# Second rows of the residual turned by DVE and DRAM at three stage boundaries

## The chip, the core and the metric

The kernel runs on one core of a Trainium2 chip. TensorE (PE) multiplies matrices from SBUF into PSUM, VectorE (DVE), ScalarE (ACT) and GpSimd (POOL) work on tiles, SyncE (SP) issues DMAs. The metric is the device time of one execution in microseconds (us); lower is better. The kernel before took 928.2 us (median of 3 runs, 925.2 to 928.4).

## What is computed

A trunk of two layers on 256 tokens of width 1024. Each layer adds half a feed-forward block to h, then a mixer (convolution in layer 0, latent attention in layer 1), then half a second feed-forward block. A last norm ends it.

```python
def rmsnorm(x, g):
    return x * lax.rsqrt(jnp.mean(x * x, axis=-1, keepdims=True) + RMS_EPS) * g

def swiglu_ffn(h, w1, w3, w2):
    return (jax.nn.silu(h @ w1) * (h @ w3)) @ w2          # 1024 -> 2816 -> 1024

def mla(h, positions, w_a, g_q, g_kv, w_uq, w_ukv, w_o):
    a = h @ w_a                                            # 1024 -> 512 + 256 + 64
    c_q = rmsnorm(a[..., :Q_LORA], g_q)
    c_kv = rmsnorm(a[..., Q_LORA:Q_LORA + KV_LORA], g_kv)
    k_rope = a[..., Q_LORA + KV_LORA:]
    q = jnp.einsum("bsc,chd->bshd", c_q, w_uq)
    kv = jnp.einsum("bsc,chd->bshd", c_kv, w_ukv)
    ...

for i in range(DEPTH):
    h = h + 0.5 * swiglu_ffn(rmsnorm(h, ffn_norm1[i]), ...)
    m = rmsnorm(h, mix_norm[i])
    h = h + (conv_module(m, ...) if i % 2 == 0 else mla(m, ...))
    h = h + 0.5 * swiglu_ffn(rmsnorm(h, ffn_norm2[i]), ...)
return rmsnorm(h, final_norm)
```

## The kernel before

**Tiles.** The 256 tokens are two row blocks, tb = 0 and 1, of 128 rows ("first rows" and "second rows"). h stands in SBUF with tokens on partitions, h[0] and h[1], each 128 by 1024. A product that sums over the width needs h with channels on partitions, so each stage starts by turning h: eight 128 by 128 tiles a row block, k = 0 to 7. The norm's gain goes in with the turned copy, and its row factor R is applied to the products.

**Products.** Every fp32 product is three fp32r products of a high and a low part (mm3): lo weights with Xh (L251), hi weights with Xh (L254), hi weights with Xl (L255). By names, Xh and Xl are the parts of the turned h, u the products of a feed-forward's first two matrices, o those of its last, a the attention's low-rank products.

**Weights.** SP loads blocks of 1 MB into one of three raw buffers (L162). ACT casts the high part (hi, L167) and DVE subtracts the low part (lo, L168), in two pieces a block, into one of five buffers. load_ahead keeps up to three blocks ahead of use.

**A stage's end.** Rows.finish runs the last two weight blocks as four groups of 12 products, in the order (tb, half of the width) = (0,0), (0,1), (1,0), (1,1). After each group DVE adds the result to h (L513 or L515), and early(i) of the next stage's Norm is called with i = 0 to 3: i = 1 turns the first half of the first rows, i = 2 their second half and starts their row factor, i = 3 turns the first half of the second rows. late() turns the last half and is called in the next stage, after the products of the first rows. A turn is split_rows: four PE transposes into one PSUM buffer of tag B (tp, L295), four ACT copies to Xh (L309), four DVE operations to Xl (L313).

**A stage's start.** The first chunk (c = 0) of ffn_in multiplies with a piece of w1 (m = 0) and of w3 (m = 1), each two weight blocks. m = 0 runs the eight k of the first rows, then the eight of the second; m = 1 follows with both. The attention (mla) starts with low-rank products of two kinds: query (512 wide) for first and second rows, then key and value with rotary key (320 wide) for first and second rows. Each is normed (normed: squares on ACT into junk, L278, powers on POOL, cn on DVE, L1046) and turned into CQ or CK by split_rows; the rotary key kd (key_rope: kx L1051, rp L1001 and L1003) is turned by a PE transpose after the query products qr.

**The gate's way.** The product of silu and gate in ffn_in is already turned without PE: DVE transposes 32 by 32 blocks inside the tile (gt, L558), SP writes four quarters to DRAM (gd, L562) and reads the tile back (gb, L564), in such an order that the blocks land where the whole transpose needs them.

**Order.** Engines work in program order as a scheduler has fixed it; functions marked urgent are put ahead of the surrounding work, and order(a, b) keeps a behind b.

## Time and profile before

| | |
|---|---|
| runs | 928.4, 928.2, 925.2 us; median 928.2 |
| profiled execution | 925.73 us; its span 923.9 us; mean granted clock 0.998 |
| weight DMA, 1 MB | 5.0 us from issue to landing (median) |
| HBM | 206 GB/s over the span |

The page gives for each engine its busy time and share of the span. The chain of waits follows back from the last instruction to what released it. Rows of groups read: line, engine, operation, output <- input, shapes, count, then busy us and mean ns of one, then the engine's idle time just before them with what ended it. Rows of the timeline read: start, length, engine, line, operation, and in brackets the idle time before. Rows by stretch read: window, length, then busy us and count of PE, PEld (weight loads), DVE, ACT and POOL, then the granted clock, DMA share and GB/s. A row of waits reads: instruction waiting <- instruction waited for, total us, times, longest.

The edited boundaries lie at about 450 to 470 us (end of layer 0's second feed-forward, start of layer 1's first), 632 to 652 (into the attention) and 733 to 746 (out of the attention).

### The profile page before, as it was taken

Reading aid. Unit: us, or ns where it says so; the run is one execution under the profiler, and the core shown is the slowest. Engines: PE = TensorE matmul, PEld = TensorE weight load, DVE = VectorE, ACT = ScalarE, POOL = GpSimd, SP = SyncE. Lnnn points to the kernel's source line nnn. Section 1 sums busy time; section 2 is a strip of 40 time slices with the busy share of each in tenths; the row PEclk is TensorE's granted clock in tenths of the full one; section 3 lists DMA queues with packets and bytes.
Section 4 is the critical chain, followed back from the end, with each engine's and each line's share of the span. In section 5 each row is a group of like instructions: output and inputs, shape, how many; then the busy total and the mean of one; then the engine's idle time right before and its main releaser. Section 6 shows DMA issues by size and latency. Waiting matters only on the chain.

```text
span 923.9 us, 12098 instructions
## 1 busy us (share of the span) xinstructions
PE 914.5 (99%) x4370; PEld 767.5 (83%) x4370; DVE 585.3 (63%) x925; ACT 493.4 (53%) x844; POOL 120.1 (13%) x255
## 2 busy tenths in 40 slices
PE   9999999999999999999999999999999999999997
PEld 7888888898978888888888888888898888888886
DVE  5895764489987666654476665544676686556633
ACT  7664443488877444543465444534666574445422
POOL 1720000079941000000000000001200000000000
PEclk9999999999999999999999999999999999999999
DMA  9886776534227767766457776753451567676711
GB/s 336 312 311 234 279 245 226 183 138 137 93 69 281 244 231 245 251 217 222 178 190 253 244 244 234 252 183 120 182 183 46 201 232 245 232 247 241 242 46 46
DMA packets 60972, 191.58 MB, mean 207 GB/s; under 512 B 11376, under 2 KB 33520, under 8 KB 41584
## 3 DMA queue, kind: packets, MB, share of 16 engines
q1 hardware_dynamic: 60336, 190.13, 58.8%
q8 instruction: 34, 0.56, 0.2%
q10 hardware_dynamic: 576, 0.69, 0.2%
q14 instruction: 26, 0.21, 0.1%
HBM read 178.20 MB, written 12.58 MB: 206 GB/s over the span
## 4 chain that ended last, share of the span: by engine, by line
PE 91%; DVE 5%; ACT 2%; issue 1%; POOL 1%; DMA 0%; POOLq 0%; ACTq 0%; DVEq 0%
PE u L251 17%; PE u L254 17%; PE u L255 17%; PE o L255 9%; PE o L254 9%; PE o L251 9%; PE gate L651 2%; DVE acc L728 2%; PE u L651 2%; PE o L892 1%; PE tp L295 1%; PE u L260 1%; DVE lo L168 1%; ACT prod L749 0%; PE sc L1133 0%
## 5 line engine op out<-in xcount | busy, mean ns | idle before, releaser
L168 DVE TENSOR_TENSOR lo<-raw,hi 128x1024 fp32r<-128x1024 f32 (+1 forms) x292 | 343.8, 1218 | 184.6 <-ACT hi L167 184.3
L167 ACT CAST hi<-raw 128x1024 fp32r<-128x1024 f32 x294 | 292.8, 1048 | 254.5 <-PE o L255 83.8
L251 PE MATMUL u<-lo,Xh 128*128 128x512 f32 x688 | 268.1, 390 | 0.0
L254 PE MATMUL u<-hi,Xh 128*128 128x512 f32 x688 | 267.7, 389 | 0.0
L255 PE MATMUL u<-hi,Xl 128*128 128x512 f32 x688 | 267.6, 389 | 0.0
L251 PEld LDWEIGHTS u<-lo,Xh 128*128 128x128 f32 x688 | 129.2, 188 | 27.0 <-DVE lo L168 0.4
L255 PEld LDWEIGHTS u<-hi,Xl 128*128 128x128 f32 x688 | 129.2, 188 | 26.9
L254 PEld LDWEIGHTS u<-hi,Xh 128*128 128x128 f32 x688 | 129.2, 188 | 26.6
L254 PE MATMUL o<-hi,Gh 128*128 128x512 f32 (+1 forms) x356 | 137.9, 387 | 0.0
L255 PE MATMUL o<-hi,Gl 128*128 128x512 f32 (+1 forms) x356 | 137.8, 387 | 0.0
L251 PE MATMUL o<-lo,Gh 128*128 128x512 f32 (+1 forms) x356 | 137.2, 387 | 0.0
L286 POOL TENSOR_TENSOR ms<-ss 128x1 f32<-128x1 f32 x16 | 8.0, 502 | 601.8 <-ACT junk L278 601.8
L251 PEld LDWEIGHTS o<-lo,Gh 128*128 128x128 f32 x356 | 66.9, 188 | 13.5
L254 PEld LDWEIGHTS o<-hi,Gh 128*128 128x128 f32 x356 | 66.9, 188 | 13.5
L255 PEld LDWEIGHTS o<-hi,Gl 128*128 128x128 f32 x356 | 66.9, 188 | 13.4
L569 DVE TENSOR_TENSOR Gl<-gb,Gh 128x512 fp32r<-128x512 f32 (+1 forms) x48 | 31.3, 651 | 51.1 <-ACT Gh L568 51.1
L568 ACT CAST Gh<-gb 128x512 fp32r<-128x512 f32 (+1 forms) x48 | 28.0, 584 | 65.2 <-DMA gb<-gd 65.2
L728 DVE SCALAR_TENSOR_TENSOR acc<-V,dw,acc 128x128 f32<-128x128 f32 (+1 forms) x176 | 54.5, 390 | 0.0
L749 ACT ACTIVATE prod<-V,dw 128x128 f32<-128x128 f32 (+1 forms) x129 | 45.8, 415 | 1.8 <-POOL Y L750 1.0
L619 DVE TENSOR_TENSOR s<-s,u 128x512 f32<-128x512 f32 (+1 forms) x48 | 30.5, 636 | 10.3 <-PE u L255 10.1
L618 ACT ACTIVATE s<-u,R 128x512 f32<-128x512 f32 (+1 forms) x48 | 31.2, 650 | 6.7 <-PE u L255 5.9
L558 DVE STREAM_TRANSPOSE gt<-s 128x512 f32<-128x512 f32 (+1 forms) x48 | 32.0, 667 | 1.5
(210 smaller groups left out, 855.8 us busy)
## 6 DMA issues: line engine op xcount, KB each, us to landing
raw<-in_f2w SPq DMA_DIRECT2D x66, 1024.0 KB, 5.0
raw<-in_f1w SPq DMA_DIRECT2D x62, 1024.0 KB, 5.0
raw<-in_cw SPq DMA_DIRECT2D x12, 1024.0 KB, 4.8
gd<-gt SPq DMA_DIRECT2D x160, 64.0 KB, 3.4
gb<-gd SPq DMA_DIRECT2D x40, 256.0 KB, 4.8
raw<-in_wo SPq DMA_DIRECT2D x4, 1024.0 KB, 4.8
raw<-in_wuq SPq DMA_DIRECT2D x3, 1024.0 KB, 4.8
raw<-in_f1w SPq DMA_DIRECT2D x8, 256.0 KB, 5.8
```

Of the source, the lines that this page charges most:

```text
L167: casts[len(loaded), i] = (nc.scalar.copy(hi[:, c], raw[:, c]), low.tensor_sub(lo[:, c], raw[:, c], hi[:, c].bitcast(F32)))
L168: low.tensor_sub(lo[:, c], raw[:, c], hi[:, c].bitcast(F32)))
L251: mm = nc.tensor.matmul(o, ah, bl, start=start, stop=False)
L254: nc.tensor.matmul(o, ah, bh, start=False, stop=False)
L255: return nc.tensor.matmul(o, al, bh, start=False, stop=stop)
L558: nc.vector.transpose(t[:, :w], g[:, :w].rearrange("p (t j q) -> p j t q", t=n, q=32))
L569: nc.vector.tensor_sub(Gl[:, f, tbs(tb)].rearrange("p t (i q) -> p t i q", q=32), bv, gh.bitcast(F32))
L618: nc.scalar.activation(s[:, :w], u[0, tb][:, :w], AF.Silu, scale=X.r[tb])
L619: nc.vector.tensor_mul(s[:, :w], s[:, :w], u[0, tb][:, w:] if both else u[1, tb])
L651: mm = nc.tensor.matmul(u[:, t], w[:, c], X.x[:, k, t], start=(k == 0), stop=(k == KT - 1))
L728: dve_last.append(nc.vector.scalar_tensor_tensor(out if j == j1 - 1 else y, v, w, y, op0=ALU.mult, op1=ALU.add))
L749: prods_last.append(nc.scalar.activation(p, v, AF.Copy, scale=w))
```

## The change

At three boundaries (into layer 1's first feed-forward, its attention, its second feed-forward) the second rows are no longer turned by split_rows. Norm gets a pool (turn_by_dma). begin(0), called with early(2), and begin(1), called with early(3), turn the halves of h[1] by turn_blocks: one DVE transpose of 32 by 32 blocks, four SP writes to DRAM, one SP read. late() calls end, which makes Xh (ACT) and Xl (DVE) from the tile read back, ordered behind the casts of the last weight block loaded so far. The gate's turn calls the same helper.

SP's loads of weight blocks not yet in use are ordered behind the last turn's read. A new first_chunk runs c = 0 of a feed-forward behind such a boundary in the order: m = 0 first rows; m = 1 first rows, k = 0 to 3; m = 0 second rows; m = 1 first rows, k = 4 to 7; m = 1 second rows. It holds all four weight blocks at once. In the attention the low-rank products run query and key for the first rows, then both for the second; the turn of the first query rows follows the last key products and that of the second follows the first rows' query products. The final norm's tiles share the new pool's buffers, and the load of its gain waits behind the turns.

```diff
--- before.py
+++ after.py
@@ -144,6 +144,9 @@
 
     casts = {}
 
+    turns = []
+    last_read = [None]
+
     def load(src, pieces=1):
         if isinstance(src, tuple):
             raw = rawp.tile([P, HB], F32, tag="raw", name=uid("raw"))
@@ -159,7 +162,10 @@
                 c = slice(i * n // pieces, (i + 1) * n // pieces) if len(loaded) < 4 else slice(n)
                 fetch(raw[:, c], src[:, c])
         else:
-            nc.sync.dma_start(raw[:, :n], src)
+            dma = nc.sync.dma_start(raw[:, :n], src)
+            if turns and len(loaded) >= n_used[0]:
+
+                order(dma, turns[-1].ins)
         for i in range(pieces):
             c = slice(i * n // pieces, (i + 1) * n // pieces)
 
@@ -316,12 +322,29 @@
                 order(low, a.ins)
         return high
 
+    def turn_blocks(pool, src, n, tag):
+
+
+        w = n * P
+        t = pool.tile([P, 512], F32, tag=tag + "t", name=uid(tag + "t"), bufs=2)
+        nc.vector.transpose(t[:, :w], src.rearrange("p (t j q) -> p j t q", t=n, q=32))
+        d = dram.tile([P, w], F32, tag=tag + "d", name=uid(tag + "d"), bufs=4)
+        dv = d.rearrange("(j p) (i c) -> i p j c", p=32, c=32 * n)
+        for i in range(4):
+            nc.sync.dma_start(dv[i], t[32 * i:32 * i + 32, :w].rearrange("p (j c) -> p j c", j=4))
+        b = pool.tile([P, 512], F32, tag=tag + "b", name=uid(tag + "b"), bufs=2)
+        last_read[0] = nc.sync.dma_start(b[:, :w], d)
+        return b[:, :w].rearrange("p (i t q) -> p t i q", i=4, q=32)
+
     class Norm:
 
 
-        def __init__(self, gname, half=False):
+        def __init__(self, gname, half=False, turn_by_dma=None):
             self.col = GCOL[gname]
             self.half = half
+
+            self.pool = turn_by_dma
+            self.turning = []
             self.whole = False
             self.xh = xp.tile([P, KT, S], F32R, tag="Xh", name=uid("Xh"))
             self.xl = xp.tile([P, KT, S], F32R, tag="Xl", name=uid("Xl"))
@@ -349,16 +372,45 @@
                 self.part(0, 0)
                 self.first_high = self.high
             elif i == 2:
+                if self.pool:
+                    self.begin(0)
                 self.part(0, 1)
                 self.rms(0)
+            elif i == 3 and self.pool:
+                self.begin(1)
             elif i == 3:
                 self.part(1, 0)
 
+        @urgent
+        def begin(self, q):
+            self.turning.append(turn_blocks(self.pool, h[1][:, 512 * q:512 * q + 512], 4, "h"))
+            turns.append(last_read[0])
+
+        @urgent
+        def end(self, q):
+
+            for j in range(4):
+                k = 4 * q + j
+                g = G[:, self.col + k:self.col + k + 1]
+                t = self.turning[q][:, j]
+                high, low = (x[:, k, tbs(1)].rearrange("p (i q) -> p i q", q=32) for x in (self.xh, self.xl))
+                both = (nc.scalar.activation(high, t, AF.Copy, scale=g),
+                        nc.vector.scalar_tensor_tensor(low, t, g, high.bitcast(F32), op0=ALU.mult, op1=ALU.subtract))
+
+                for i in range(PIECES):
+                    for ins, cast in zip(both, casts[len(loaded) - 1, i]):
+                        order(ins, cast.ins)
+
         def late(self):
 
-            if not self.whole:
+            if self.whole:
+                return
+            if self.pool:
+                for q in range(2):
+                    self.end(q)
+            else:
                 self.part(1, 1)
-                self.rms(1)
+            self.rms(1)
 
     @urgent
     def first_rows(X):
@@ -445,18 +497,19 @@
 
     class Final:
         def __init__(self, act):
-            self.act = act
             self.gf = act.tile([P, D], F32, tag="gf", name="gf")
-            nc.sync.dma_start(self.gf, gfin.partition_broadcast(P))
+            order(nc.sync.dma_start(self.gf, gfin.partition_broadcast(P)), turns[-1].ins)
 
             self.e = [None] * NT
             self.n = [0] * NT
             self.y = {}
+            self.pieces = 0
 
         def piece(self, tb, c):
 
             n = c.stop - c.start
-            t = self.act.tile([P, 512], F32, tag="hg", name=uid("hg"), bufs=4)
+            self.pieces += 1
+            t = rows.tile([P, 512], F32, tag="hb" if self.pieces % 2 else "ht", name=uid("hg"), bufs=2)
             q = small.tile([P, 1], F32, tag="fq", name=uid("fq"))
             junk = tmp.tile([P, 512], F32, tag="s", name=uid("junk"))
 
@@ -552,21 +605,33 @@
         Gl = act.tile([P, NF, S], F32R, tag="Gl", name=uid("Gl"))
         def turn(c, tb, w, g):
 
-
             n = w // P
-            t = act.tile([P, 512], F32, tag="gt", name=uid("gt"), bufs=2)
-            nc.vector.transpose(t[:, :w], g[:, :w].rearrange("p (t j q) -> p j t q", t=n, q=32))
-            d = dram.tile([P, w], F32, tag="gd", name=uid("gd"), bufs=4)
-            dv = d.rearrange("(j p) (i c) -> i p j c", p=32, c=32 * n)
-            for i in range(4):
-                nc.sync.dma_start(dv[i], t[32 * i:32 * i + 32, :w].rearrange("p (j c) -> p j c", j=4))
-            b = act.tile([P, 512], F32, tag="gb", name=uid("gb"), bufs=2)
-            nc.sync.dma_start(b[:, :w], d)
             f = slice(4 * c, 4 * c + n)
-            bv = b[:, :w].rearrange("p (i t q) -> p t i q", i=4, q=32)
+            bv = turn_blocks(act, g[:, :w], n, "g")
             gh = Gh[:, f, tbs(tb)].rearrange("p t (i q) -> p t i q", q=32)
             nc.scalar.copy(gh, bv)
             nc.vector.tensor_sub(Gl[:, f, tbs(tb)].rearrange("p t (i q) -> p t i q", q=32), bv, gh.bitcast(F32))
+
+        def first_chunk(X, u):
+
+            kn = HB // 512
+            parts = [weights(2, False) for m in range(2)]
+            for m in range(2):
+                for tb in range(NT):
+                    u[m, tb] = bank("A", "u")
+            last = None
+            for n, (m, tb, ks) in enumerate(((0, 0, range(8)), (1, 0, range(4)), (0, 1, range(8)), (1, 0, range(4, 8)),
+                                             (1, 1, range(8)))):
+                if n == 2:
+                    X.late()
+                elif n == 3:
+                    load_ahead()
+                for k in ks:
+                    hi, lo = parts[m][k // kn]
+                    c = slice(k % kn * 512, k % kn * 512 + 512)
+                    mm = mm3(u[m, tb], X.xh[:, k, tbs(tb)], X.xl[:, k, tbs(tb)], hi[:, c], lo[:, c], k == 0,
+                             k == KT - 1, (last,) if last is not None and k == ks[0] else ())
+                last = mm
 
         for c in range(6):
 
@@ -574,7 +639,9 @@
             w = 256 if both else 512
             kn = HB // 512
             u = {}
-            for m in range(1 if both else 2):
+            if c == 0 and X.pool:
+                first_chunk(X, u)
+            for m in range(0 if u else 1 if both else 2):
                 parts = weights(KT // kn, c > 0 or m > 0)
                 if X.whole and c == 0 and m == 0:
                     load_to(4)
@@ -1027,14 +1094,17 @@
         nc.gpsimd.memset(mk, 0.0)
         nc.gpsimd.memset(mk[0:1, :], -1e30)
 
-        def low(parts, w, tb):
+        last_low = [None]
+
+        def low(parts, w, tb, last):
             u = bank("A", "a")
             for a in range(2):
                 hi, lo = parts[a]
                 for j in range(4):
                     k = 4 * a + j
-                    mm3(u[:, :w], X.xh[:, k, tbs(tb)], X.xl[:, k, tbs(tb)], hi[:, j * w:(j + 1) * w],
-                        lo[:, j * w:(j + 1) * w], k == 0, k == KT - 1)
+                    last_low[0] = mm3(u[:, :w], X.xh[:, k, tbs(tb)], X.xl[:, k, tbs(tb)], hi[:, j * w:(j + 1) * w],
+                                      lo[:, j * w:(j + 1) * w], k == 0, k == KT - 1,
+                                      (last,) if last is not None and k == 0 else ())
             return u
 
         @urgent
@@ -1054,20 +1124,24 @@
                 rope(act, kd[:, i, :], kx.rearrange("p (n i f) -> p n i f", n=1, i=2), 1, cc, sn, tb)
             return kd.rearrange("p i f -> p (i f)")
 
-        parts = weights(2, False)
+        parts = [weights(2, False) for _ in range(2)]
         cq, ck, kd = [], [], []
+        last = None
         for tb in range(NT):
-            u = low(parts, QL, tb)
-            if tb == 0:
-                X.late()
-                load_ahead()
-            cq.append(normed(u, QL, tb))
-        parts = weights(2)
-        for tb in range(NT):
-            u = low(parts, KVL + ROPE, tb)
-            ck.append(normed(u, KVL, tb))
-            kd.append(key_rope(u, tb))
-            split_rows(cq[tb], 0, 4, GCOL["q"], CQh, CQl, tb)
+            for i, w in enumerate((QL, KVL + ROPE)):
+                u = low(parts[i], w, tb, last)
+                last = last_low[0]
+                if tb == 0 and i == 1:
+                    X.late()
+                elif tb == 1 and i == 0:
+                    load_ahead()
+                if i == 0:
+                    cq.append(normed(u, QL, tb))
+                else:
+                    ck.append(normed(u, KVL, tb))
+                    kd.append(key_rope(u, tb))
+                if tb == 1 and i == 1:
+                    split_rows(cq[0], 0, 4, GCOL["q"], CQh, CQl, 0)
 
 
         QR = act.tile([P, 4, S], F32, tag="QR", name="QR")
@@ -1096,6 +1170,7 @@
                 mm3(u, CQh[:, k, tbs(tb)], CQl[:, k, tbs(tb)], hi[:, k * 512:(k + 1) * 512],
                     lo[:, k * 512:(k + 1) * 512], k == 0, k == 3)
             if tb == 0:
+                split_rows(cq[1], 0, 4, GCOL["q"], CQh, CQl, 1)
                 for t in range(NT):
                     split_rows(ck[t], 0, 2, GCOL["kv"], CKh, CKl, t)
             q = act.tile([P, 512], F32, tag="cn512", name=uid("qrope"), bufs=2)
@@ -1220,10 +1295,11 @@
         pass
     X = conv(X, lambda act: Norm("ffn2_0", half=True))
     apart.close()
-    X = ffn(X, lambda act: Norm("ffn1_1", half=True))
-    X = ffn(X, lambda act: Norm("mix_1"))
+    rows = ctx.enter_context(tc.tile_pool(name="rows", bufs=1))
+    X = ffn(X, lambda act: Norm("ffn1_1", half=True, turn_by_dma=rows))
+    X = ffn(X, lambda act: Norm("mix_1", turn_by_dma=rows))
     cc, sn = rope_tables()
-    X = mla(X, lambda act: Norm("ffn2_1", half=True), cc, sn)
+    X = mla(X, lambda act: Norm("ffn2_1", half=True, turn_by_dma=rows), cc, sn)
     ffn(X, Final)
 
 
```

## The prediction

> **What bounds the kernel now.** I read the page first, then TensorE's waits, then busy time by stretch.
>
> ```profile
> PE 914.5 (99%) x4370; PEld 767.5 (83%) x4370; DVE 585.3 (63%) x925; ACT 493.4 (53%) x844; POOL 120.1 (13%) x255
> ...
> PE 91%; DVE 5%; ACT 2%; issue 1%; POOL 1%; DMA 0%; POOLq 0%; ACTq 0%; DVEq 0%
> ```
> ```profile
> PE warm L243 <- DVE still L238: 1.0, 1, 1.0
> PE ms L766 <- ACT sq L760: 0.8, 1, 0.8
> PE u L260 <- ACT hi L378: 0.6, 1, 0.6
> PE nope L251 <- DVE rp L1003: 0.4, 1, 0.4
> ```
> ```profile
> 450.00:475.00 25.00, 25.00 (x120) 20.67 (x119) 15.93 (x28) 15.58 (x34) 2.35 (x8) 1.00 0.34 123
> ...
> 670.00:680.00 10.00, 9.62 (x81) 9.39 (x80) 10.00 (x25) 8.54 (x17) 0.00 (x0) 1.00 0.29 106
> ...
> 735.00:750.00 15.00, 15.00 (x76) 12.45 (x75) 11.40 (x24) 14.22 (x32) 2.33 (x8) 1.00 0.32 118
> 900.00:923.90 23.90, 17.67 (x90) 14.94 (x88) 7.82 (x14) 4.64 (x12) 2.23 (x7) 0.91 0.12 44
> ```
>
> TensorE (PE) is busy 99% of the span, 91% of the chain of waits is its own, and it waits for another engine four times, 2.8 us together. The stretch rows (length, then busy PE, PEld, DVE, ACT, POOL, then the granted clock) show the stages around the first and third edited boundary without a gap, at clock 1.00. Only 670 to 680, inside the attention, has a gap, and there DVE is busy for all 10.00 us. So a change pays only if it takes instructions from PE, and it costs whatever new wait it gives PE.
>
> **What it removes.** Twelve rows of four transposes stand at the three boundaries; six go, those of the second row block. In the chain (start, length):
>
> ```profile
> 459.17 0.44 PE tp L295 x4
> ...
> 462.13 0.44 PE tp L295 x4
> 462.57 0.23 PE u L251
> ...
> 465.80 0.44 PE tp L295 x4
> ```
> ```profile
> 736.60 0.87 PE tp L295 x8
> ```
>
> Four transposes take 0.44 us of the chain, so one takes 0.11, and 24 take **2.6 us**. That is the whole possible gain, 0.28% of 925.73. ACT's four Xh and DVE's four Xl for each set stay; they only read from a DRAM-turned tile instead of PSUM.
>
> **What it adds at a boundary, first one worked.** DVE turns 32 by 32 blocks, SP issues four writes and a read, for each of the two halves. The same helper already runs for the gate, which gives its prices.
>
> ```profile
> L558 DVE STREAM_TRANSPOSE gt<-s 128x512 f32<-128x512 f32 (+1 forms) x48 | 32.0, 667 | 1.5
> ```
> ```profile
> L562 SPq DMA_DIRECT2D gd<-gt x46: 302/432/502, 759.2 to 859.9; - x46
> ...
> DMA to landing us min/median/max: 1.6/3.5/5.7
> ```
> ```profile
> L564 SPq DMA_DIRECT2D gb<-gd x10: 319/329/338, 763.9 to 852.4; - x10
> ...
> DMA to landing us min/median/max: 2.6/3.9/5.1
> ```
> ```profile
> 458.59 0.75 DVE L515 SCALAR_TENSOR_TENSOR h<-o,rh,h 128x512 f32<-128x512 f32 x1 [2.04 <-POOL R L289]
> ...
> 461.22 1.13 DVE L313 SCALAR_TENSOR_TENSOR Xl<-tp,G,Xh 128x128 fp32r<-128x128 f32 x4 [1.88 <-ACT Xh L309]
> 462.26 0.74 DVE L515 SCALAR_TENSOR_TENSOR h<-o,rh,h 128x512 f32<-128x512 f32 x1
> ...
> 466.27 1.14 ACT L309 ACTIVATE Xh<-tp,G 128x128 fp32r<-128x128 f32 x4 [1.91 <-PE tp L295]
> ```
>
> A transpose costs DVE about 0.7 us. Three write issues at 0.43 put the last of four 1.3 us after the first. To landing (shortest, median, longest), a write takes 1.6, 3.5, 5.7, a read 2.6, 3.9, 5.1. The short values belong to a queue with nothing in front, the long ones to one with 1 MB weight blocks in it. I take the short ones: the edit also orders the look-ahead weight blocks behind the turn's read, so nothing is in front.
>
> Second half, which is the late one: add 462.26 to 463.0; DVE then has the four Xl of the first rows (1.1), then the transpose, done at 464.8; last write issued 466.1, landed 467.7; read landed 470.3; ACT's first Xh at about 470.7. When is it needed? The first half serves k = 0 to 3, the second k = 4 to 7. The stage's products start at 462.13 (the transposes there are gone) and cost 0.23 each. Ahead of the second rows stand 24 products of the first factor and 12 of the second: 36 x 0.23 = 8.3 us, so k = 0 is due at 470.4 and k = 4, twelve products later, at 473.2. Slack 2.5 us for the second half; the first half, added at 458.59 and ready by the same steps at about 466, has 4. So **no stall at boundary 1**, with this cover: 36 products of the first rows. With medians for both transfers it would be ready at 473.9 (stall 0.7), with the longest at 477.3 (4.1): bounds 0 to 4.1. The delayed weight blocks cost nothing: four blocks for both factors are loaded before the turns, and the next chunk's are not used until 64 more products (14 us) have passed.
>
> Boundary 2 is the same chain, with 24 products at 0.23 and 24 narrower ones ahead of the second rows: more cover, 0 again (0 to about 3).
>
> **Boundary 3.** Its four adds end within 3.2 us (734.13 to 737.33 below), so both turns come close together.
>
> ```profile
> 734.13 2.05 DVE L513 TENSOR_TENSOR h<-o,h 128x512 f32<-128x512 f32 x3 [0.79 <-PE o L255]
> 736.64 0.69 DVE L513 TENSOR_TENSOR h<-o,h 128x512 f32<-128x512 f32 x1 [0.46 <-PE o L255]
> 737.25 1.11 DVE L313 SCALAR_TENSOR_TENSOR Xl<-tp,G,Xh 128x128 fp32r<-128x128 f32 x4
> ...
> 745.79 1.28 ACT L618 ACT_TABLE_LOAD   x1
> ```
>
> On DVE a transpose (0.7) now stands ahead of the last add and of the first rows' Xl of this row, while PE starts 0.44 earlier; the third product waits: **0.5 us** (0 to 1.1). Second rows are then due at 737.04 + 0.5 + 8.3 = 745.8. SP queues both sets of writes ahead of both reads, so the first read issues near 740.8 and lands near 743.4, the second near 745.1 (due at 748.6); but ACT first finishes the table load and a silu that wait for the first rows' products (737.04 + 0.5 + 24 x 0.23 = 743.1; + 1.28 + 0.7 = 745.0), Xh at 745.4. Covered by 0.4 us, which is thin; bounds 0 to 3.3.
>
> **Inside the attention** the rest of the edit moves more than the turns do. Low-rank products now run first rows (query, key), then second rows (query, key); the query rows' transposes follow later. In the changed program's order PE has, after the key products: 12 query products, transposes of the second query rows and of both key rows, two query products, the transpose of the rotary key, then the next query product.
>
> ```profile
> 667.53 0.37 ACT L278 ACTIVATE junk<-a,R 128x128 f32<-128x128 f32 x1 [3.85 <-DVE kd L1005]
> ...
> 668.42 0.19 POOL L286 TENSOR_TENSOR ms<-ss 128x1 f32<-128x1 f32 x1 [3.36 <-ACT junk L278]
> ...
> 669.83 0.48 DVE L1046 TENSOR_SCALAR cn<-a,rr 128x256 f32<-128x256 f32 x1 [2.27 <-POOL rr L1044]
> 670.23 0.28 DVE L1051 TENSOR_SCALAR kx<-a,R 128x64 f32<-128x64 f32 x1
> 670.42 2.35 DVE L168 TENSOR_TENSOR lo<-raw,hi 128x1024 fp32r<-128x1024 f32 x2
> 672.68 0.22 DVE L1001 TENSOR_TENSOR rp<-kx,cc 128x64 f32<-128x64 f32 x1
> ...
> 673.36 1.12 DVE L313 SCALAR_TENSOR_TENSOR CKl<-tp,G,CKh 128x128 fp32r<-128x128 f32 x4
> ```
>
> Norm to cn takes 2.8 us here (667.53 to 670.3); PE brings 12 x 0.23 + 6 x 0.11 = 3.4 less the semaphore steps, and cn stands behind a cast: wait 0.3. Then ACT's first copy of the turned query rows: 0.25. The rotary key's transpose needs the PSUM buffer that two CKl give back, and ahead of them DVE has kx (0.2) and two lo casts (2.3); with CKl 0.55 that is 3.05 after cn, against about 1.0 of PE work: wait 2.0. The next query product needs the low part of the turned rows, behind six rp (0.7): wait 0.6. Together **3.15 us**; bounds 1 (DVE ahead by one cast) and 5.5 (one more cast pair waiting). The 0.4 of the old wait at L251 goes, since by then DVE is past its rotary work. Each of five new waits also breaks the overlap of a weight load:
>
> ```profile
> 664.14 0.19 PEld L255 LDWEIGHTS qr<-hi,CQ 128*128 128x128 f32 x1 [0.26 <-DVE CQ L313]
> 664.16 0.48 PE L255 MATMUL qr<-hi,CQ 128*128 128x512 f32 x1
> ...
> 664.48 0.39 PE L251 MATMUL qr<-lo,CQ 128*128 128x512 f32 x1
> ```
>
> After this stalled load the next product starts 0.32 later (664.16 to 664.48) in place of 0.23: 0.1 each, in all 0.5.
>
> The end of the kernel is unchanged: the gain vector's load and the tiles' new tags lie far before the last pieces.
>
> **Sum:** -2.6 - 0.4 + 0.5 + 3.15 + 0.5 = +1.15 us: 925.73 becomes 926.9 for the profiled execution (span 923.9). That execution lies 2.5 below the median of the runs (928.2; 925.2 to 928.4); the mean of these four times is 926.9, and I set the sum on it: **928.1**.
>
> The granted clock is 1.00 in all stretches but the last, where PE idles 6.2 us and it is 0.91. The Trainium skill ("TensorE: Matmul & The Clock Gate", Part 1 and "HAM oscillation") puts the gate at an idle window of about 3.4 us; but it also tells of a kernel whose many short idles between groups made the clock swing. By the first the sum stays; by the second, one window at half clock after the attention's waits would add some 1.7 us, an estimate from that page, 929.8. The trace's waits up to 1.0 us left no mark in the clock; none here shows 3 us of waits close together.
>
> **Rivals.** (a) *All hidden.* DVE reaches CKl earlier than I think and PE never waits: -2.6 - 0.4 on 926.9, **923.9**. For it: windows at 100% with DVE at 63% overall. Against it: DVE at 10.00 of 10 in 670 to 680. (b) *The round trip through DRAM is the new wait, on the slower side.* If transfers run at the loaded values, PE waits for the second rows in each boundary: at medians 0.7 + 0 + 0.2, at the longest 4.1 + 3 + 3.3 = 10.4. It decides from 2.5 us of extra latency at boundary 1 and 0.4 at boundary 3; halfway between the ends it costs 5.5, 933.6. For it: the gate's turns, by the same helper, have these medians. Against it: those share the queue with weights, which the new order keeps away. (c) *It doesn't do what it says*: the removed transposes were worth nothing, because the ends of PE's instructions are modelled and the products around them don't really move; then +1.15 + 2.6, 930.7. Against: in the chain the products' starts stand 0.44 apart around each set.
>
> **Chances.** Forecast 0.56, (a) 0.16, (b) 0.20, (c) 0.08. 0.5%, 4.6 us, is about what a measurement of this kernel can tell from no change. Faster by more than that needs more than all that is removed: 0.04, left for runs that differ by 3 us. Slower by more: (b) for the most part and a little of (c) and the clock, 0.22. The rest, 0.74, within. The likeliest's own range is 925.5 to 931; with (a) below and (b) up to its halfway price, **924 to 934**.
>
> **What would show it.** Right: 24 fewer transposes; stretches around 462 to 475 still full; waits of PE on DVE of about 2 and 0.6 us near 664, and 0.5 near 738; new waits nowhere else. Wrong if PE waits on ACT's Xh made from the DRAM tile (b), if no wait appears at the rotary key's transpose (a), or if the clock falls below 1.00 after 660.

## The result and the profile after

| | before | after |
|---|---|---|
| median of the runs of this comparison, us | 925.38 (925.20 to 928.40, 6 runs) | 932.22 (931.25 to 932.84, 6 runs) |
| profiled execution, us | 925.73 | 932.56 |
| its span, us | 923.9 | 930.8 |
| its mean granted clock | 0.998 | 0.991 |

The change makes the kernel slower: after over before is 1.0063, with a 95% interval of 1.0046 to 1.0079. The forecast was 928.1, beside a median of 928.2 before.

The page of the changed kernel, first part, then its list of what TensorE waited for (engine, operation and line, releaser, then us in total, times, longest):

```profile
PE 917.0 (99%) x4346; PEld 768.8 (83%) x4346; DVE 590.2 (63%) x931; ACT 495.5 (53%) x844; POOL 125.5 (13%) x255
```
```profile
PE tp L301 <- DVE cn L1116: 2.8, 2, 2.0
PE tp L301 <- DVE CKl L319: 1.4, 1, 1.4
...
PE qr L261 <- DVE CQ L319: 0.5, 1, 0.5
PE u L261 <- DVE Xl L319: 0.3, 1, 0.3
```

The 24 transposes are gone (4370 to 4346), yet PE is busy for 2.5 us more. That can't be more work; it is less work, part of it at a lower clock. Three of the waits are new and lie in the attention (cn, CKl, CQ, 4.7 us together); one, of 0.3, is at the third boundary. No wait names Xh made from the DRAM-turned tile.

Next the stretches of the changed kernel that answer to the prediction's, with the one between the third adds ahead of boundaries 1 and 2 (length, busy PE, PEld, DVE, ACT, POOL, granted clock, DMA share, GB/s):

```profile
459.36:640.28 180.92, 180.92 (x806) 149.81 (x805) 107.03 (x125) 86.15 (x116) 4.15 (x8) 1.00 0.65 225
```
```profile
660.00:670.00 10.00, 7.02 (x35) 5.23 (x33) 8.65 (x14) 8.53 (x22) 5.80 (x8) 0.88 0.75 242
670.00:680.00 10.00, 8.29 (x35) 7.19 (x36) 9.11 (x26) 3.21 (x6) 0.00 (x0) 0.60 0.77 283
...
735.00:750.00 15.00, 14.69 (x71) 11.96 (x70) 9.24 (x18) 7.37 (x20) 2.22 (x6) 1.00 0.18 50
900.00:930.80 30.80, 24.31 (x119) 20.44 (x117) 8.27 (x15) 4.64 (x12) 2.25 (x7) 0.94 0.09 35
```

The whole stage behind boundary 1 is full, at clock 1.00. The attention from 660 to 680 is neither: PE idles 4.7 of 20 us, and the clock is 0.88 and then 0.60, where before it was 1.00. In single microseconds:

```profile
664.00:665.00 1.00, 0.60 (x3) 0.18 (x1) 0.50 (x1) 0.46 (x1) 0.83 (x3) 1.00 0.68 107
665.00:666.00 1.00, 0.00 (x0) 0.00 (x0) 0.23 (x1) 1.00 (x2) 0.83 (x4) 1.00 0.79 311
666.00:667.00 1.00, 0.42 (x4) 0.43 (x5) 1.00 (x2) 0.53 (x1) 0.84 (x3) 1.00 1.08 459
667.00:668.00 1.00, 0.45 (x5) 0.21 (x2) 0.92 (x2) 0.73 (x3) 0.70 (x1) 0.85 0.41 172
668.00:669.00 1.00, 0.72 (x3) 0.73 (x4) 1.00 (x3) 0.93 (x4) 0.00 (x0) 0.50 0.73 98
...
677.00:678.00 1.00, 1.00 (x6) 0.90 (x5) 0.92 (x2) 0.00 (x0) 0.00 (x0) 0.53 0.45 139
678.00:679.00 1.00, 1.00 (x8) 0.88 (x7) 0.19 (x1) 0.19 (x1) 0.00 (x0) 1.00 0.97 410
```

From 664 to 668 PE is busy for 1.47 of 4 us, in pieces; at 667.7 the clock falls to 0.50 and stays there until 678, some 10 us, the last five of which PE is busy throughout.

To see which stage lost the time, the residual adds on DVE serve as marks in every kernel: the third add of a sublayer is followed by the boundary. In the changed kernel:

```profile
459.36 0.75 DVE L568 SCALAR_TENSOR_TENSOR h<-o,rh,h 128x512 f32<-128x512 f32 x1 [2.04 <-POOL R L295]
...
640.28 0.75 DVE L568 SCALAR_TENSOR_TENSOR h<-o,rh,h 128x512 f32<-128x512 f32 x1 [2.48 <-PE o L261]
...
741.07 2.06 DVE L566 TENSOR_TENSOR h<-o,h 128x512 f32<-128x512 f32 x3 [0.78 <-PE o L261]
```
and in the kernel before (458.59 and 734.13 stand in the prediction):
```profile
640.48 0.75 DVE L515 SCALAR_TENSOR_TENSOR h<-o,rh,h 128x512 f32<-128x512 f32 x1 [2.48 <-PE o L255]
```

| us from mark to mark | before | after | difference |
|---|---|---|---|
| start to the third add ahead of boundary 1 | 458.59 | 459.36 | +0.77 |
| to the third add ahead of boundary 2 (boundary 1 lies in it) | 181.89 | 180.92 | -0.97 |
| to the first add behind the attention (boundary 2 lies in it) | 93.65 | 100.79 | +7.14 |
| to the end of the span (boundary 3 lies in it) | 189.77 | 189.73 | -0.04 |

The first row is code that the change doesn't touch. The stretch of before, then that of after, in which it comes up:

```profile
250.00:255.00 5.00, 4.81 (x41) 4.58 (x41) 4.82 (x19) 3.50 (x14) 4.28 (x11) 1.00 0.11 13
```
```profile
250.00:255.00 5.00, 4.89 (x29) 4.81 (x29) 3.52 (x14) 2.59 (x10) 4.00 (x10) 0.66 0.00 0
```

The clock was 1.00 in the one and 0.66 in the other, and in the kernels below, with the same code there, this first mark lies anywhere from 458.14 to 459.82. It is taken for a difference between executions. What is to be explained is +7.14 in the attention.

The chain of waits of the changed kernel there (start, length, what):

```profile
660.76 0.57 ACT junk L284 x2
661.40 3.16 POOL ms L292
...
665.74 0.16 POOL ms L292
...
666.88 0.84 POOL rr L1114
...
668.14 0.28 DVE kx L1121
668.41 2.27 DVE lo L174 x2
670.68 0.52 DVE CKl L319 x2
```

It isn't PE's own for more than ten microseconds. It runs over the norm of the second query rows on POOL, the norm of the second key rows on POOL, two casts on DVE, and CKl. One step is odd: the first ms adds two columns of one element a partition, and takes 3.16 us; its next instance takes 0.16 of the chain. DVE's timeline of the same kernel tells what stood beside it, and the timelines of before (POOL, then DVE) show that the same thing had been there:

```profile
661.00 3.50 DVE L174 TENSOR_TENSOR lo<-raw,hi 128x1024 fp32r<-128x1024 f32 x3
665.77 0.75 DVE L1116 TENSOR_SCALAR cn<-a,rr 128x512 f32<-128x512 f32 x1 [1.27 <-POOL rr L1114]
```
```profile
662.65 1.23 POOL L286 TENSOR_TENSOR ms<-ss 128x1 f32<-128x1 f32 x1 [4.14 <-ACT junk L278]
```
```profile
659.21 4.62 DVE L168 TENSOR_TENSOR lo<-raw,hi 128x1024 fp32r<-128x1024 f32 x4
```

In both kernels POOL's add ends 0.05 us after DVE's run of lo casts does: 661.40 + 3.16 = 664.56 against 661.00 + 3.50 = 664.50, and 662.65 + 1.23 = 663.88 against 659.21 + 4.62 = 663.83. POOL seems held while DVE runs them. The Trainium skill ("SBUF — State Buffer", "Who interferes with whom") has a rule for it: a DVE instruction with two inputs in SBUF contends with a GpSimd instruction that reads SBUF, and the later one waits. The casts read raw and hi, and the trace agrees, with 3.16 us against 0.19. By the trace POOL can wait for more than the one cast that was running.

### The profile page after: what moved, and what is told of

It reads as the page before. It is cut to its first block, busy times and chain, and to the rows that moved or that the text cites. A ratio compares the mean times of both kernels' runs of the same rounds, so it can differ in the third digit from the quotient of the medians.

```text
span 930.8 us, 12107 instructions
## 1 busy us (share of the span) xinstructions
PE 917.0 (99%) x4346; PEld 768.8 (83%) x4346; DVE 590.2 (63%) x931; ACT 495.5 (53%) x844; POOL 125.5 (13%) x255
## 4 chain that ended last, share of the span: by engine, by line
PE 93%; ACT 2%; DMA 1%; DVE 1%; POOL 1%; issue 1%; SPq 0%; POOLq 0%; ACTq 0%; DVEq 0%
PE u L261 17%; PE u L260 17%; PE u L257 17%; PE o L261 9%; PE o L260 9%; PE o L257 9%; PE u L718 3%; PE gate L718 3%; PE o L959 1%; PE u L266 1%; PE tp L301 1%; PE pairs L761 1%; PE nope L257 1%; PE nope L261 1%; PE nope L260 1%; PE sc L1208 1%
## 5 line engine op out<-in xcount | busy, mean ns | idle before, releaser
L292 POOL TENSOR_TENSOR ms<-ss 128x1 f32<-128x1 f32 x16 | 10.9, 680 | 602.9 <-ACT junk L284 602.9
L817 POOL TENSOR_TENSOR odd<-odd,prod 128x128 f32<-128x128 f32 (+1 forms) x62 | 33.0, 536 | 0.0
```

The source lines that it names most:

```text
L817: pool_last.append(nc.gpsimd.tensor_tensor(o, o, p, op=ALU.add))
```

## The experiments

Three theories were open: the attention's new order costs the time (its waits, and the clock that falls with them); the turn through DRAM costs it (transfers, SP's queue, DVE's extra work); and, as a finer form of the first, it is DVE's lo casts, which hold POOL and stand ahead of the norms and CKl. Each kernel is set against runs of the kernel before that were taken beside its own. The stage time given is that from the third add ahead of boundary 2 to the first add behind the attention (93.65 before, 100.79 after); like the waits and the rows, it is from one profiled execution of each kernel.

**The attention as before, the turns at boundaries 1 and 3 kept.**

```diff
-            for i, w in enumerate((QL, KVL + ROPE)):
-                u = low(parts[i], w, tb, last)
...
+            u = low(parts, QL, tb)
+            if tb == 0:
+                X.late()
+                load_ahead()
+            cq.append(normed(u, QL, tb))
...
-    X = ffn(X, lambda act: Norm("mix_1", turn_by_dma=rows))
+    X = ffn(X, lambda act: Norm("mix_1"))
```

> This is the changed kernel with the attention of before: its low-rank products in the old order and its second rows turned by TensorE; the turns through DRAM stay at the two boundaries into feed-forwards. Theory A (the whole loss comes from the attention's new order: about 5 us of TensorE waits between 664 and 672 us, plus some 4 us from the half clock that follows): two of three boundaries gain 0.87 us each, less a wait of 0.3 us at the third boundary, so 1.4 us faster than before, ratio 0.998 to 0.999; granted clock 1.00 from 660 to 680 us, no wait of a transpose over 0.5 us. Theory B (the turns through DRAM themselves cost time, through their DMAs or through late second rows): still slower than before, ratio over 1.002.

Measured: 925.29 us (924.22 to 927.53, 10 runs) against 925.53, ratio 0.9993 [0.9982, 1.0004], which can't be told from no change; span 922.5, 1.4 under before, of which 0.43 lies ahead of the first mark, in code that is the same. Stages: 180.93, 93.67, 189.74. Its row of 670 to 680 is that of before again:

```profile
670.00:680.00 10.00, 9.62 (x81) 9.38 (x80) 10.00 (x24) 9.15 (x16) 0.00 (x0) 1.00 0.37 120
```

So the loss lies in the attention's part of the edit alone, and boundary 1 keeps its gain of 0.96 without it. POOL's add is held for 1.23 us here too, and PE doesn't wait: what was a harmless hold became a wait.

**The new order alone, every turn on TensorE.** This is the kernel before with the attention's part of the diff, so boundary 2 costs its transposes again.

```diff
-        parts = weights(2, False)
+        parts = [weights(2, False) for _ in range(2)]
...
+            for i, w in enumerate((QL, KVL + ROPE)):
+                u = low(parts[i], w, tb, last)
...
+                split_rows(cq[1], 0, 4, GCOL["q"], CQh, CQl, 1)
```

> This is the kernel before with only the attention's new order; TensorE turns all rows. Theory A: the waits and the half clock are there without any turn through DRAM, and the 2.6 us of transposes aren't saved: 7 to 9.5 us slower than before, ratio 1.0075 to 1.010, granted clock about 0.5 for some 10 us near 668. Theory B: the attention's waits came from second rows that arrived late through DRAM, so without those the ratio is 1.000 to 1.002 and the clock stays 1.00.

Measured: 932.48 us (932.26 to 933.84, 4 runs), ratio 1.0069 [1.0053, 1.0086]; stage 100.70, clock 0.66 in 670 to 680. The loss is there without a single turn of h through DRAM. It is a little smaller than expected: the stage has eight transposes (0.9 us) more than in the changed kernel, but its waits come to 4.3 us (cn 1.8, CKl 2.2, CQ 0.3) in place of 4.7. POOL, then DVE, of this kernel:

```profile
664.39 2.13 POOL L286 TENSOR_TENSOR ms<-ss 128x1 f32<-128x1 f32 x1 [7.42 <-ACT junk L278]
```
```profile
664.11 2.36 DVE L168 TENSOR_TENSOR lo<-raw,hi 128x1024 fp32r<-128x1024 f32 x2
```

Again POOL's add ends 0.05 us after the casts (666.52 against 666.47).

**TensorE kept busy in the first wait.** 16 products on zeroes are put ahead of the second query rows' transposes; they change no output.

```diff
             if tb == 0:
-                split_rows(cq[1], 0, 4, GCOL["q"], CQh, CQl, 1)
+                warm = keep_warm(16, after=last)
+                split_rows(cq[1], 0, 4, GCOL["q"], CQh, CQl, 1, after=(warm,))
```

> The changed kernel with 16 products of no use (128x256, written to a spare PSUM bank) on TensorE between the first rows' query products and the transposes of the second query rows, where it waits 2.0 us. If the half clock follows from TensorE's idling (theory A), it stays at 1.00 through 667 to 678 us while the waits on DVE's cn and CKl stay about as long; about 4 us faster than the changed kernel, ratio to before about 1.002. If the clock falls for another cause, it is still about 0.5 near 668 and the time is that of the changed kernel or up to 1 us more, ratio 1.0065 to 1.008.

Measured: 931.07 us (929.94 to 933.09, 4 runs) against 925.53, ratio 1.0057 [1.0041, 1.0074]; stage 99.79. The clock does follow TensorE's idling: it is at half speed for some 3.2 us (670.9 to 674.1) in place of 10. But the kernel gains only 1.0 us, not the 4 expected. The wait at cn shrinks to 1.4, and the one at CKl grows from 1.4 to 2.7: DVE is late anyway, and in this kernel it also runs four rotary products (rp, 0.7 us) ahead of CKl, which stand behind it in the changed kernel.

**TensorE kept busy in all three waits** (16, 8 and 20 such products), to price the clock by itself.

```diff
+                warm = keep_warm(16, after=last)
+                turned = []
+                split_rows(cq[1], 0, 4, GCOL["q"], CQh, CQl, 1, after=(warm,), turned=turned)
+                split_rows(ck[0], 0, 2, GCOL["kv"], CKh, CKl, 0, after=(warm,), turned=turned)
+                warm = keep_warm(8, after=turned[-1])
+                split_rows(ck[1], 0, 2, GCOL["kv"], CKh, CKl, 1, after=(warm,), turned=turned)
+                warm = keep_warm(20, after=turned[-1])
```

> The changed kernel with products of no use in all three of the attention's waits (16, 8 and 20 of 128x256), DVE's order of casts ahead of cn and CKl left as it is. This prices the half clock apart from the waits. If the clock's fall is the larger part of the loss (about 4 us of 7), the clock is 1.00 from 660 to 680 us and the stage takes under 97.5 us; if DVE's order is the larger part and the half clock mostly covers time in which TensorE would wait anyway, the clock is 1.00 too but the stage still takes 98.5 to 100 us.

Measured: 930.38 us (929.35 to 930.54, 4 runs) against 926.9, ratio 1.0038 [1.0025, 1.0051]; stage 98.17, which lies between what the two theories gave. Its row:

```profile
670.00:680.00 10.00, 9.45 (x69) 8.55 (x68) 10.00 (x28) 4.01 (x7) 0.00 (x0) 1.00 0.63 228
```

The clock is 1.00 throughout 660 to 690, and POOL's add is still held for 3.04 us. The products of no use don't lengthen the waits: the query product behind the last wait starts 31.9 us after the third add in both kernels (672.19 - 640.28 and 671.56 - 639.70). From there the changed kernel ran 5.7 us at half clock. So half speed costs about 100.79 - 98.17 = 2.6 us of the 7.14, and 4.5 remain with the clock restored.

**The lo casts of two weight blocks behind the second query norm on DVE.**

```diff
+        def lows_behind_norm():
+            for n in (len(loaded) - 2, len(loaded) - 1):
+                for i in range(PIECES):
+                    order(casts[n, i][1], last_cn[0].ins)
...
                     cq.append(normed(u, QL, tb))
+                    if tb == 1:
+                        lows_behind_norm()
```

> The changed kernel with DVE's lo casts of the last two loaded weight blocks ordered behind the second query rows' cn. If GpSimd's first step of the norm's power (ms, 3.15 us in the changed kernel, 0.2 elsewhere) is held up by DVE's back-to-back lo casts, it takes about 0.2 us now, cn starts near 662.8 in place of 665.8 us, and the wait of 2.0 us before the second query rows' transposes goes; the casts then stand ahead of the key's cn, so a wait of 3 to 4 us comes there in its place and the total stays within 2 us of the changed kernel. If the long step has another cause, ms still takes about 3 us and cn starts no earlier than 665.5.

Measured, in one run: 931.39 us against 925.53, span 929.6, stage 100.83. The casts moved past the one norm and onto the next. POOL's timeline, and DVE's casts:

```profile
660.54 0.19 POOL L292 TENSOR_TENSOR ms<-ss 128x1 f32<-128x1 f32 x1 [5.23 <-ACT junk L284]
...
663.13 0.75 POOL L292 TENSOR_TENSOR ms<-ss 128x1 f32<-128x1 f32 x1 [1.22 <-ACT junk L284]
663.96 1.05 POOL L293 TENSOR_SCALAR ms<-ms 128x1 f32<-128x1 f32 x1
665.10 1.41 POOL L295 TENSOR_TENSOR r<-ms,neghalf 128x1 f32<-128x1 f32 x1
666.58 0.70 POOL L1114 TENSOR_TENSOR rr<-r,R 128x1 f32<-128x1 f32 x1
```
```profile
662.61 4.62 DVE L174 TENSOR_TENSOR lo<-raw,hi 128x1024 fp32r<-128x1024 f32 x4
```

This is the test of the hold. With DVE free, the query's add takes 0.19 us; beside four casts, the key's four steps take 0.75, 1.05, 1.41 and 0.70 us, where they took 0.19, 0.19, 0.55 and 0.19 before. The time didn't improve: the waits are now 2.5 us for ACT's CQ, and 2.3 for CKl.

**The casts later still**: of one block behind the second query norm's cn, of two more behind the last CQ and CKl.

```diff
+                    if tb == 1:
+                        lows_behind(len(loaded) - 2, last_cn[0])
...
                     split_rows(ck[t], 0, 2, GCOL["kv"], CKh, CKl, t)
+                for n in (1, 2):
+                    lows_behind(len(loaded) - n, last_split[0])
```

> The changed kernel, all three turns and the attention's new order kept; only DVE's order in the attention differs: the casts lo of one block stand behind the second query rows' cn, and those of the next two blocks behind the low parts CQ and CKl of the turned rows. Theory C (the attention's loss is DVE's order: casts of blocks that aren't needed yet stand ahead of cn, CKl and CQ, and hold up GpSimd's norm beside it; the half clock only follows from these waits): TensorE's waits on cn, CKl and CQ fall from 4.7 us to under 2 us, the granted clock stays at 1.00, and the stage from the third add before the attention to the first add after it takes 94 to 96.5 us in place of 100.8; ratio to before 1.000 to 1.003. Theory D (the products themselves come too early in the new order, whatever DVE does): waits stay over 4 us and the stage over 99 us; ratio over 1.005.

Measured: 927.70 us (926.54 to 929.56, 10 runs) against 926.44, ratio 1.0018 [1.0007, 1.0028]; stage 95.61, clock 1.00 from 660 to 690. Its waits in the attention:

```profile
PE tp L301 <- DVE cn L1119: 2.4, 1, 2.4
...
PE tp L301 <- DVE CKl L319: 0.6, 1, 0.6
...
PE qr L261 <- DVE CQ L319: 0.2, 1, 0.2
```

With PE's order up to the last of these waits as in the changed kernel, moving casts on DVE takes away 5.2 of the 7.14 us. The waits left, 3.2 us, are more than the "under 2" expected, and they close the sum: 3.2 less the 0.9 of eight transposes and the 0.4 of the old wait is +1.9, against 95.61 - 93.65 = +1.96.

The wait of 2.4 that is left is no longer for the second query rows (their add takes 0.19 and PE doesn't wait for their cn) but for the second key rows, and POOL is held there again (POOL, then DVE):

```profile
663.48 0.75 POOL L292 TENSOR_TENSOR ms<-ss 128x1 f32<-128x1 f32 x1 [1.22 <-ACT junk L284]
664.32 1.05 POOL L293 TENSOR_SCALAR ms<-ms 128x1 f32<-128x1 f32 x1
```
```profile
662.97 2.35 DVE L174 TENSOR_TENSOR lo<-raw,hi 128x1024 fp32r<-128x1024 f32 x2
```

Two steps that take 0.19 us each when free take 1.4 us more here.

**The query's up-projection of the first rows between the two low-rank products of the second rows**, so that PE has work while the norms run.

```diff
                     cq.append(normed(u, QL, tb))
+                    if tb == 1:
+                        split_rows(cq[0], 0, 4, GCOL["q"], CQh, CQl, 0)
+                        load_ahead(1)
+                        uq.append(query(wq, 0, last))
...
+                    turned_query(uq[0], 0, low_cq)
+                    uq.append(query(wq, 1, last))
```

> All three turns through DRAM, but another order in the attention: low-rank query and key products of the first rows, query products of the second, then the first rows' up-projected query products ahead of the second rows' key products, the second query rows' transposes in the middle of those, and the key rows' transposes after the products that need the query alone. Cover for the second rows stays 9 us. If theory C holds, the stage takes 92.5 to 94 us (93.65 in the kernel before, less 0.88 for the eight transposes, and up to 1 us of short waits), the clock stays 1.00, and the whole is 1 to 2.2 us faster than before, ratio 0.9975 to 0.999. If the turn into the attention costs something of its own that the other runs hid, the stage takes over 95 us.

Measured: 932.67 us (930.08 to 933.39, 6 runs) against 926.44, ratio 1.0061 [1.0045, 1.0077]; stage 100.17. A miss: the wait for cn is down to 0.3, but PE waits 2.8 for CKl and 1.3 for CQ, the clock falls again (0.72 in 680 to 690), and the same pair stands in the trace, ten microseconds later (POOL, then DVE):

```profile
672.10 2.79 POOL L292 TENSOR_TENSOR ms<-ss 128x1 f32<-128x1 f32 x1 [7.75 <-ACT junk L284]
```
```profile
672.49 2.35 DVE L174 TENSOR_TENSOR lo<-raw,hi 128x1024 fp32r<-128x1024 f32 x2
```

**The key rows turned after the query's products, the casts behind cn, CQ and CKl.**

```diff
+                    wq, = weights()
+                    uq = query(wq, 0)
+                    split_rows(cq[1], 0, 4, GCOL["q"], CQh, CQl, 1, after=(last_low[0],))
+                    ck.append(normed(u, KVL, tb, last_split[:1]))
...
+        high = split_rows(ck[1], 0, 2, GCOL["kv"], CKh, CKl, 1, after=first_pair[:1])
+        for n in (1, 2):
+            lows_behind(len(loaded) - n, last_split[0], high)
```

> All three turns through DRAM. In the attention the low-rank products keep the changed order, but what follows stands as in the kernel before: both query products, then the products that need the query alone, and only then the transposes of the second key rows and of the rotary keys; on DVE every cast lo that isn't needed by then stands behind cn, CQ and CKl. Theory C (the loss is DVE's and TensorE's order behind the low-rank products, not the turn): waits on cn, CKl and CQ together under 1 us, clock 1.00, stage 92.8 to 94.3 us (93.65 before, less 0.88 for eight transposes), the whole 1 to 2 us faster than before, ratio 0.998 to 0.999. If the new order of the low-rank products costs something by itself, the stage stays over 95 us.

Measured: 927.80 us (926.16 to 931.84, 12 runs) against 926.9, ratio 1.0014 [1.0002, 1.0025]; stage 97.16, where less than 94.3 was expected. Another miss, of a different kind: the waits for CQ come to 0.9 and those for cn and CKl are gone, but a later one is new:

```profile
PE o L257 <- ACT Oh L1270: 1.9, 1, 1.9
```

The wait went on to the attention's output products. In ACT's timeline the cast that makes Oh stands right behind four hi casts:

```profile
717.30 3.88 ACT L173 CAST hi<-raw 128x1024 fp32r<-128x1024 f32 x4
721.08 0.37 ACT L1270 CAST Oh<-pv 128x256 fp32r<-128x256 f32 x1
```

Moving them wasn't tried. The clock then falls to 0.50, from 722.1 to 725.7 (3.6 us, of which half, 1.8, is lost). With it the 3.5 us (97.16 - 93.65) are nearly accounted for: waits of 2.8 less the old 0.4, less 0.9 for eight transposes, and 1.8 for the clock make 3.3.

No version beats the kernel before by more than the measurement tells apart. The best is the first, with the attention left as it was.

## Why the prediction was wrong

**What held.** At boundary 1 the turn was priced rightly. A write of 64 KB and a read of 256 KB had these times to landing, shortest, median and longest, in the two tiles' rows of the changed kernel (hd, then hb):

```profile
DMA to landing us min/median/max: 1.6/1.8/3.5
```
```profile
DMA to landing us min/median/max: 2.6/2.7/3.2
```

The medians stand near the short values that were chosen, 1.6 and 2.6, not near the gate's 3.5 and 3.9. That the look-ahead blocks wait behind the turn is the likely reason; no run has the turn without it. In ACT's timeline, Xh of boundary 1 came when it was said to come:

```profile
466.94 1.28 ACT L397 ACTIVATE Xh<-hb,G 128x128 fp32r<-128x128 f32 x4 [1.44 <-DMA hb<-hd]
...
471.36 1.28 ACT L397 ACTIVATE Xh<-hb,G 128x128 fp32r<-128x128 f32 x4 [2.19 <-DMA hb<-hd]
```

Predicted were about 466 and 470.7; with the 0.77 by which this execution was late at the add, 466.8 and 471.5. PE didn't wait, and the stage is 0.97 shorter against the 0.88 of eight transposes. The same stage takes 180.92 or 180.93 in every kernel with this turn and 181.87 in the one run without it (the new order alone). So at this boundary both the rival of the round trip (933.6, near the measured time by its number, but by the wrong mechanism) and the one by which the removed transposes were worth nothing fell. Boundary 2 shows no gain: with the new order its stage takes 100.79 with the turn and 100.70 without, and no run has the turn there without waits.

**Boundary 3, a small miss.** The wait for Xl is 0.3 (0.5 was predicted), and Xh isn't waited for. Yet the last stage gains 0.04 in place of 0.88 - 0.5 = 0.38. In the last stretch PE idles 30.80 - 24.31 = 6.49 us where it idled 6.23; that is another 0.26, and the rest, 0.88 - 0.31 - 0.26 - 0.04 = 0.27, wasn't found.

**The step that failed: the waits inside the attention, 3.15 us with 0.5 for weight loads, at clock 1.00.** For the stage, with -0.88 for the transposes and -0.4 for the old wait, that was +2.4; it measured +7.14. By its own parts:

- *cn of the second query rows*: the prediction puts six transposes behind the query products and gives this cn no wait and no price. PE waited 2.0 for it. In the kernel before, this norm took 2.8 us from the second junk on ACT to the end of cn (656.50 to 659.29); in the changed kernel it took 5.7 (660.76 to 666.52). POOL's add was held for 3.16 and three casts stood ahead of cn on DVE (661.00 to 664.50). DVE sat idle for the last 1.27 ahead of cn, so the hold cost at most 1.27, and DVE's own casts, which stood there until 664.50, the rest. ACT too was late: it began this norm 1.8 us behind its products. With the casts later it was no earlier, and yet PE didn't wait for this cn.
- *cn of the second key rows*: predicted 0.3, measured 0.8. The one cast that the prediction put ahead of it is there (666.44, 1.22 us), and beside it POOL's last step takes 0.84 in place of 0.19. The norm was priced from the row of before in which POOL's add took 0.19 (668.42); the norm of the first key rows, six microseconds earlier in the same trace, had the add at 1.23 beside DVE's casts, and the prediction doesn't use that row.
- *CKl*: predicted 2.0, measured 1.4, by the mechanism named (kx and two lo casts ahead of it). *CQ*: 0.6 predicted, 0.5 measured. *ACT's copy*: 0.25 predicted, no wait listed. The 0.5 for weight loads wasn't measured by itself.
- *The clock*: predicted to stay; "if the clock falls below 1.00 after 660" was a sign named of being wrong, and it fell. The 1.7 us given for one window at half clock is the nearest thing in the prediction; measured were about 2.6, over 10 us. The Trainium skill ("TensorE: Matmul & The Clock Gate", Part 1) speaks of an idle window of about 3.4 us. The same page, in "A second HAM failure mode: psum-queue depth-cycling", has a kernel in which short idles between groups of products made the clock swing. Here the longest single wait was 2.0 us, and the fall came 3.1 us after PE ran dry at 664.6, with 0.9 us of transposes in between. With the key rows turned later it fell 0.6 us after the end of a lone wait of 1.9; with the casts later it stayed at 1.00 through a wait of 2.4, with PE busy for 0.7 of the 3.1 us around it. So neither the length of the longest wait nor PE's share of some 3 us decides it in these traces, and what does stays open.

The 7.14 us come apart by three kernels: 2.6 for the clock (100.79 to 98.17, kept busy in the waits), 2.6 for the place of DVE's casts (98.17 to 95.61, casts later), 2.0 for the waits that are left even then (95.61 to 93.65), in which POOL's hold beside two casts takes up to 1.4 again. The steps are from different kernels, not strictly nested, and from one execution each. The medians of the runs, 6.84, 3.48 and 1.26 us over the kernel before, give 3.4 and 2.2 for the first two shares. How much is POOL held and how much DVE's queue can't be told apart: a version with the norm's steps taken off POOL wasn't tried.

**The number.** The sum gave +1.15, and a further 1.2 came from setting it on the mean of four runs instead of on the profiled execution. The stage miss, 7.14 - 2.4 = 4.8, outweighs both. The chance of 0.22 for slower by over 0.5% was put mainly on DRAM transfers, that is on the part of the edit which proved harmless. That 932.22 lies inside 924 to 934 is luck: the upper part of that range stands for the round trip through DRAM at its halfway price, which didn't happen.

## What to carry to other kernels

An edit that reorders products to hide a new latency is to be priced at the other end of the reorder first: list what each small step of the norm stands behind on its engine, and what runs beside it on another. A step's duration is to be taken from all its instances in the trace, above all the longest, since a hold that is covered today is the wait of tomorrow. Where new waits of one to two microseconds would stand close together, price the clock as well. And the turn through DRAM at boundary 1, with no weight blocks ahead of it in the queue and eight microseconds of cover, gave PE no wait, but it is worth only the TensorE time that it removes, there 0.1%; at boundary 3 the stage gained 0.04 us.

## What the runs showed of the hardware

- An add of one column on POOL takes 0.19 us, and 1.23, 2.13, 2.79, 3.04 and 3.16 us beside runs of DVE operations with two inputs in SBUF. In each of these it ends 0.05 us after the last of the run. In another kernel the norm's four steps went in one by one between four casts (0.75, 1.05, 1.41 and 0.70 us).
- TensorE's clock fell to half 3.1 us after PE ran dry; in these 3.1 us PE was busy for 0.9 us, and no single wait was over 2.0 us. It came back some 10 us later, five of which PE had been busy throughout; products of no use in the waits kept it at 1.00. It also fell after a lone wait of 1.9 us in one kernel, and stayed at 1.00 through one of 2.4 us in another.
- Identical code ran at clock 1.00 and at 0.66 in one stretch of 5 us (250 to 255) of two executions, with 0.77 us between them at the next mark.
